# Smaller portions of top-k work beside each expert chunk (UPUMP 2.7 to 1.1) in a one-core decoder block

## The chip, the cores and the metric

The kernel runs on one core of one Trainium2 chip. A core has a matrix engine (PE; its weight loads are shown apart as PEld), three engines for elementwise work (DVE or VectorE, ACT or ScalarE, POOL or GpSimd), and a queue that only starts transfers (SP). Each engine works through its own list of instructions; semaphores tie the lists together. The metric is the time of one execution in microseconds on the device; lower is better. All compared runs use the same inputs.

## The reference

One decoder block for 512 tokens of width 1024 in float32. First come a gated MLP, a sliding window attention and a merge of the two; the change does not touch them. Then comes the PEER layer, a retrieval over 128 x 128 = 16384 experts of one neuron each, with 8 heads and 16 experts per head and token:

```python
q = (xb @ w_pq).reshape(-1, PEER_HEADS, PEER_QDIM)
q1, q2 = q[..., :PEER_HALF], q[..., PEER_HALF:]
s1 = jnp.einsum('thd,hkd->thk', q1, sub_k1)
s2 = jnp.einsum('thd,hkd->thk', q2, sub_k2)
v1, i1 = lax.top_k(s1, PEER_TOPK)
v2, i2 = lax.top_k(s2, PEER_TOPK)
cand = (v1[..., :, None] + v2[..., None, :]).reshape(-1, PEER_HEADS, PEER_TOPK * PEER_TOPK)
sc, ci = lax.top_k(cand, PEER_TOPK)
e = (take(i1, ci // PEER_TOPK) * PEER_NKEYS + take(i2, ci % PEER_TOPK))
g = jax.nn.softmax(sc, axis=-1)
act = jax.nn.gelu(jnp.einsum('thkd,td->thk', peer_u[e], xb))
return jnp.einsum('thk,thkd->td', g * act, peer_v[e])
```

A gate, a residual sum and a layer norm follow.

## The kernel before, in words

For the first 384 tokens the kernel does not gather experts. It computes the activations of all 16384 experts densely, in 128 chunks of 128 experts, and weighs them with a tensor G that is zero except at the chosen experts. A chunk has two halves. `U_chunk(i)` loads a 512 KB tile of peer_u, splits it into a high part (`hiU`, ACT, line 451) and a low part (`loU`, raw minus high), and multiplies: 24 products of 384 columns on PE, three for each of 8 slices, high by high, high by low of the tokens, and low by high (lines 63 to 65). `V_chunk(i)` loads 512 KB of peer_v, splits it in the same way (`hiV`, `loV`), forms the weighted activations `wf`, `wh`, `wl` from the activations and G, and adds 18 products of 512 columns to six accumulators (lines 776 to 780).

`load_split2` makes the low part on POOL (line 457) while `last["pool"]` is true, and on DVE (line 459) from then on. It turns false in `end_topk`, which stands in a list of background work, `bg`, behind the top-k of all heads. This list holds Python generators. `pump(us)` adds `us` to a credit and takes work from the list until the credit is used up; each step names its price in microseconds (1.02 for the best 16 of one row, for example). So the credit decides which piece of top-k is written beside which chunk in the program, and how many chunks are written before the switch.

The order of the program is: the queries and scores, with `pump(QPUMP)`; then chunks with their low parts on POOL, with `pump(UPUMP + 1.2)` each, as long as the top-k lasts, their activations sent out to DRAM (`spilled`); then 21 chunks whose activations stay in SBUF (`res`), beside which `spread()` builds G on DVE, ACT and PE (one-hot tiles `oh`, products `psg` of lines 650 and 651, `stg`) and writes it to DRAM; some more spilled chunks; then the V halves of the 21 kept chunks; then U and V of the rest, in pairs; and at the end the V halves of all spilled chunks, whose activations come back from DRAM as `ar`, four chunks at a time.

The last 128 tokens go another way, `gather()`: their experts' rows are fetched with indirect DMAs that POOL issues (`ru`, line 665, then `rv`, line 676; 128 of each), and DVE multiplies them (lines 667 and 682). These DMAs read the list of experts `idx`, which DVE writes in one instruction, line 662, at the end of top-k. The steps are handed out with `pump_gather`: GR = 1.1 for each kept chunk's V, GUV = 2.9 for each pair, and what is then left of 260, spread evenly, over the spilled chunks. A row is a 128 x 1024 float32 tile, and four are in flight.

The kernel is written through a framework that places instructions on each engine's list with an estimate of its own of when each will be ready. So a list can hold an instruction earlier than the program text has it. Of the calls that the prediction speaks of, the text has:

```python
            U_chunk(i, False)
            spilled.append(i)
            pump(UPUMP + 1.2 * bool(last.get("pool")))
```
```python
    left = 260 - n_g
            pump_gather(left / (len(spilled) - 6))
```

Of the kernel before, what the change touches and what calls it, by code (L numbers as in the profile page):

```python
# [30 lines left out]
FPOOL = {0: 2, 1: 2, 2: 0, DENSE: 0}  # L31
UPUMP = 2.7
GUV = 2.9
# [22 lines left out]
def block_kernel(ctx, tc, I, out):  # L56
# [53 lines left out]
    with ExitStack() as fr:  # L110
# [22 lines left out]

# [1 line left out]
        cs = wp.tile([P, D], F32, name="cs")  # L135
# [23 lines left out]

        # the first column blocks of the projection build up while the modulation comes in  # L160
        wf4 = Split(big(fp, "C", "w4hi"), big(fp, "D", "w4lo"))
# [15 lines left out]
        first = [I["w_k"], I["w_v"], I["w_q"][0], I["w_q"][1]]  # L177
# [21 lines left out]

# [1 line left out]
        att = ExitStack()  # L201
# [19 lines left out]

        # keys j of a block: those of the block itself where j <= q, those of the one before where j > q
        mcur = ap_.tile([P, P], F32, name="mcur")
# [66 lines left out]

# [1 line left out]
        vln = fp.tile([P, NT, D], F32, name="vln", tag="F", bufs=1)  # L292
        w = None
        for n in range(NT):
            for gh in range(4):
                attn_group(n, gh)
                u = 4 * n + gh
# [7 lines left out]
        att.close()  # L305
# [1 line left out]
        sp_ = ExitStack()  # L307
# [32 lines left out]

# [1 line left out]
        gp = fr.enter_context(tc.tile_pool(name="gp", bufs=1, reuse_waits="tile"))  # L342
        part = big(keep, "E", "part", F32)
        for j in range(NK):
# [3 lines left out]
            for i in range(16 + 4 * j, 20 + 4 * j):  # L348
# [10 lines left out]
                   gp.tile([P, NK, S], F32R, name="mTlo"))  # L359
        # rows of 1 + gt1, 1 + gt2 and h2's scale and shift: turned, then spread to all partitions by DMA  # L360
        m4 = gp.tile([P, 4, NK], F32, name="m4")
# [24 lines left out]

# [1 line left out]
        xhat = keep.tile([P, NT, D], F32, name="xhat", tag="E", bufs=1)  # L388
# [10 lines left out]
        for hh in range(2):  # L399
            for t in range(NT):  # L400
# [13 lines left out]
                for kh in range(2):  # L414
                    pt = bank("tr", 2, f"ptx{t}{kh}")
                    hf = gp.tile([P, 4, P], F32, name=f"hf{t}{kh}", tag="hf", bufs=2)
                    for k4 in range(4):
                        k = 4 * kh + k4
                        nc.tensor.transpose(pt[:, k4 * P:(k4 + 1) * P], xhat[:, t, k * P:(k + 1) * P], ident)
                    for k4 in range(4):  # L420
                        k = 4 * kh + k4
                        if k < NEV:
                            nc.scalar.activation(hf[:, k4, :], pt[:, k4 * P:(k4 + 1) * P], AF.Identity,
                                                 scale=G2c[:, k:k + 1], bias=B2c[:, k:k + 1])
# [5 lines left out]
                    nc.vector.tensor_sub(h2T.lo[dst], hf, h2T.hi[dst].bitcast(F32))  # L430
# [1 line left out]
    pw = ctx.enter_context(tc.tile_pool(name="pw", bufs=1, reuse_waits="tile"))  # L432
# [3 lines left out]
    last = {}  # L436

    def behind(ins, other):
        """keeps ins behind other in the queue of their engine"""
        tc.add_manual_dep(ins.ins, other.ins.name,  # L440
                          mybir.DependencyInfo(mybir.DependencyClass.NoSync, mybir.DependencyReason.DATA))
# [24 lines left out]

    # background work on the vector engine, given out in portions beside the dense products
    bg = []
# [10 lines left out]

# [1 line left out]
    def raw_row(nm):  # L481
# [18 lines left out]

# [1 line left out]
    tk = ExitStack()  # L502
# [34 lines left out]
    def topk(nm, n, src, dst):  # L537
        """src(half, j): the scores of lane j of n; dst(tensor): where the lanes' 16 choices go"""
        def tl(what, shape, dt):
            return tp.tile(shape, dt, name=f"{what}{nm}", tag=f"{what}_{n}", bufs=2 if n == DENSE else 1)  # L540
        v = [tl(f"v{i}", [P, n, 16], F32) for i in range(2)]
        ix = [tl(f"ix{i}", [P, n, 16], U32) for i in range(2)]
        for half in range(2):
            for j in range(n):
                top16(v[half][:, j, :], ix[half][:, j, :], src(half, j), P, f"{nm}{half}{j}")
                yield 1.02
        # candidates (a, b) in order; a pair outside the rows has 16 or more before it that are no smaller
        cand = tl("cand", [P, n, 17, 8], F32)
        nc.vector.tensor_tensor(cand[:, :, 0:2, :].rearrange("p t a b -> p t (a b)"), v[1],
                                v[0][:, :, 0:1].to_broadcast([P, n, 16]), op=ALU.add)  # L550
        nc.vector.tensor_tensor(cand[:, :, 2:17, :], v[0][:, :, 1:16].unsqueeze(3).to_broadcast([P, n, 15, 8]),
                                v[1][:, :, 0:8].unsqueeze(2).to_broadcast([P, n, 15, 8]), op=ALU.add)
        yield 0.12 + 0.14 * n
        sc = dst(scs)
        pos = tl("pos", [P, n, 16], U32)
        for j in range(n):
            top16(sc[:, j, :], pos[:, j, :], cand[:, j].rearrange("p a b -> p (a b)"), 136, f"c{nm}{j}")
            yield 1.06
        # positions to (a, b), then the keys they stand for
        r = tl("r", [P, n, 16], U32)  # L560
        ab = [tl(f"ab{i}", [P, n, 16], F16) for i in range(2)]
        nc.vector.tensor_scalar(r, pos, 3, None, op0=ALU.logical_shift_right)
        nc.vector.tensor_scalar(ab[0], r, 1, 0, op0=ALU.subtract, op1=ALU.max)
        nc.vector.scalar_tensor_tensor(ab[1], ab[0], 1.0, ab[0], op0=ALU.min, op1=ALU.add)
        nc.vector.scalar_tensor_tensor(ab[1], ab[1], -8.0, pos, op0=ALU.mult, op1=ALU.add)
        yield 0.4
        for i, to in ((0, i1s), (1, i2s)):
            ixf = tl("ixf", [P, n, 16], F16)
            nc.vector.tensor_copy(ixf, ix[i])
            oh = tl("ohl", [P, 16, n * 16], F16)  # L570
            nc.vector.tensor_tensor(oh, io16[:, :, 0:16 * n],
                                    ab[i].rearrange("p t k -> p (t k)").unsqueeze(1).to_broadcast([P, 16, 16 * n]),
                                    op=ALU.is_equal)
            o4 = oh.rearrange("p j (t k) -> p j t k", t=n)
            nc.vector.tensor_mul(o4, o4, ixf.rearrange("p t j -> p j t").unsqueeze(3).to_broadcast([P, 16, n, 16]))
            yield 0.2 + 0.42 * n
            for m in (8, 4, 2):
                nc.vector.tensor_add(oh[:, 0:m, :], oh[:, 0:m, :], oh[:, m:2 * m, :])
            nc.vector.tensor_add(dst(to), oh[:, 0, :].rearrange("p (t k) -> p t k", t=n),
                                 oh[:, 1, :].rearrange("p (t k) -> p t k", t=n))  # L580
            yield 0.2 + 0.14 * n
# [20 lines left out]

# [1 line left out]
    def spread():  # L604
# [52 lines left out]

# [1 line left out]
    wg = gat.tile([P, P], F32, name="wg")  # L659
# [83 lines left out]
    def load_G(run):  # L743
        """weights for a run of at most 8 neighbouring chunks"""
        g = vs["vp"].tile([P, SD // TG, 8, TG], F32, name=f"G{run[0]}", tag="G", bufs=2)
# [215 lines left out]
```

## Time and profile before

| what | value |
|---|---|
| time, median of 3 runs | 1770.31 us (1767.48 to 1774.57) |
| span of the profiled execution, first to last instruction | 1769.1 us |
| PE busy | 1666.7 us, 94% of the span |
| DVE, ACT, POOL busy | 1342.3, 751.4 and 450.3 us |
| moved by DMA | 413.82 MB, 234 GB/s over the span |
| granted TensorE clock, mean | 0.981 of full speed |

The profile is of one execution, and no time other than its span is given for it; the span lies 1.2 us under the median. A busy PE is not a PE at its peak, since matmuls are pipelined and overlap in the profile. An engine's idle time is shown with what ended it, and idle time of an engine that nobody waits for costs nothing.

### The profile page before, as it was taken

The page shows a single profiled execution, that of the slowest core. Times are in us where ns is not written, and L with a number is a line of the kernel's source. Part 1 is how long each engine was busy: PE and PEld are TensorE (multiplying, and loading weights), DVE is VectorE, ACT ScalarE, POOL GpSimd, SP SyncE. Part 2 cuts the span into 40 slices and gives each one's busy share as a digit, 9 for nine tenths or more (in the row PEclk, how much of TensorE's full clock was granted, in tenths as well). Part 3 has the DMA queues.
Part 4 walks back from the last instruction along what each step waited for, and adds up shares of the span by engine and source line. Part 5 has one row for each costly group of instructions (what it writes and reads, how often), then busy time and mean ns, then how long its engine had stood idle before and what let it go on. Part 6 is the DMA issues. An engine that isn't in the chain of part 4 may idle for free.

```text
span 1769.1 us, 23554 instructions
## 1 busy us (share of the span) xinstructions
PE 1666.7 (94%) x8658; PEld 1444.7 (82%) x8658; DVE 1342.3 (76%) x2483; ACT 751.4 (42%) x1171; POOL 450.3 (25%) x321
## 2 busy tenths in 40 slices
PE   5999989999999991888999999999999999999997
PEld 3866778788788991788898899999999999999886
DVE  6466786444469999787978777878878878888776
ACT  3467632233523330888843333333333333333343
POOL 2000000000133541000012444444454554554002
PEclk9999999999999995999999999999999999999999
DMA  7502267542332341656799999999989989999972
GB/s 269 189 1 72 103 217 245 190 149 83 108 104 84 131 156 35 240 211 224 257 337 334 349 319 335 349 313 343 343 305 334 356 310 347 324 322 358 296 236 76
DMA packets 164837, 413.82 MB, mean 234 GB/s; under 512 B 24849, under 2 KB 75313, under 8 KB 161394
## 3 DMA queue, kind: packets, MB, share of 16 engines
q1 hardware_dynamic: 127330, 277.79, 45.7%
q0 software_dynamic: 36960, 134.50, 21.3%
q8 instruction: 67, 1.10, 0.2%
q14 instruction: 48, 0.39, 0.1%
q10 hardware_dynamic: 432, 0.04, 0.0%
HBM read 379.04 MB, written 32.98 MB: 233 GB/s over the span
## 4 chain that ended last, share of the span: by engine, by line
PE 46%; issue 2%; DVE 1%; ACT 1%; POOL 1%; DMA 0%; DVEq 0%; POOLq 0%; ACTq 0%
PE acc L779 9%; PE acc L780 9%; PE acc L776 9%; PE psU L65 7%; PE psU L63 7%; PE psU L64 7%; ACT stg L652 1%; POOL ru L665 1%; DMA ru<-in_peer_u_dram,idx 0%; ACT oh L640 0%; DVE oh L642 0%; DVE xhat L707 0%; DVE oh L635 0%; DVE xhat L715 0%; DVE ru L667 0%
## 5 line engine op out<-in xcount | busy, mean ns | idle before, releaser
L65 PE MATMUL psU<-h2Thi,loU 128*128 128x384 f32 x1008 | 340.1, 337 | 38.0 <-DVE loU L459 38.0
L63 PE MATMUL psU<-h2Thi,hiU 128*128 128x384 f32 x1008 | 340.5, 338 | 0.0
L64 PE MATMUL psU<-h2Tlo,hiU 128*128 128x384 f32 x1008 | 339.7, 337 | 0.0
L780 PE MATMUL acc<-hiV,wl 128*128 128x512 f32 x768 | 300.3, 391 | 0.0
L779 PE MATMUL acc<-loV,wh 128*128 128x512 f32 x768 | 300.1, 391 | 0.0
L776 PE MATMUL acc<-hiV,wh 128*128 128x512 f32 x768 | 298.6, 389 | 1.2 <-ACT wh L761 1.2
L665 POOL DMA_INDIRECT ru<-in_peer_u_dram,idx x128 | 155.5, 1215 | 466.3 <-DVE ru L667 410.2
L459 DVE TENSOR_TENSOR loV<-rawV,hiV 128x1024 fp32r<-128x1024 f32 x128 | 156.6, 1224 | 117.1 <-ACT hiV L451 116.9
L451 ACT ACTIVATE hiV<-rawV 128x1024 fp32r<-128x1024 f32 x128 | 135.3, 1057 | 242.1 <-PE psU L64 224.2
L676 POOL DMA_INDIRECT rv<-in_peer_v_dram,idx x128 | 181.9, 1421 | 209.1 <-DVE facc L682 185.7
L65 PEld LDWEIGHTS psU<-h2Thi,loU 128*128 128x128 f32 x1008 | 190.5, 189 | 38.3 <-DVE loU L459 38.3
L451 ACT ACTIVATE hiU<-rawU 128x1024 fp32r<-128x1024 f32 x126 | 133.7, 1062 | 169.6 <-PE acc L780 75.2
L64 PEld LDWEIGHTS psU<-h2Tlo,hiU 128*128 128x128 f32 x1008 | 190.7, 189 | 3.0
L63 PEld LDWEIGHTS psU<-h2Thi,hiU 128*128 128x128 f32 x1008 | 190.5, 189 | 3.0
L780 PEld LDWEIGHTS acc<-hiV,wl 128*128 128x128 f32 x768 | 144.1, 188 | 30.4 <-DVE wl L762 0.3
L776 PEld LDWEIGHTS acc<-hiV,wh 128*128 128x128 f32 x768 | 144.2, 188 | 29.8 <-ACT wh L761 1.5
L779 PEld LDWEIGHTS acc<-loV,wh 128*128 128x128 f32 x768 | 144.1, 188 | 28.7 <-DVE loV L459 0.3
L682 DVE SCALAR_TENSOR_TENSOR facc<-rv,wg,facc 128x1024 f32<-128x1024 f32 x126 | 159.3, 1279 | 9.5 <-DMA rv<-in_peer_v_dram,idx 9.3
L761 ACT ACTIVATE wh<-wf 128x384 fp32r<-128x384 f32 x128 | 67.1, 526 | 216.3 <-DVE wf L757 112.8
L667 DVE SCALAR_TENSOR_TENSOR ru<-ru,h2n 128x1024 f32<-128x1024 f32 x128 | 154.3, 1221 | 5.6 <-DMA ru<-in_peer_u_dram,idx 5.6
L459 DVE TENSOR_TENSOR loU<-rawU,hiU 128x1024 fp32r<-128x1024 f32 x108 | 131.5, 1220 | 5.7 <-ACT hiU L451 5.7
L457 POOL TENSOR_TENSOR lopq<-rawpq,hipq 128x1024 fp32r<-128x1024 f32 x16 | 39.2, 2452 | 323.2 <-ACT hipq L451 323.2
(626 smaller groups left out, 2946.5 us busy)
## 6 DMA issues: line engine op xcount, KB each, us to landing
rawU<-in_uT_dram SPq DMA_DIRECT2D x128, 512.0 KB, 5.0
rawV<-in_peer_v_dram SPq DMA_DIRECT2D x128, 512.0 KB, 6.0
wa<-in_w_ada_dram SPq DMA_DIRECT2D x48, 512.0 KB, 4.3
Gd<-stg SPq DMA_DIRECT2D x24, 1024.0 KB, 3.9
G<-Gd SPq DMA_DIRECT2D x13, 1536.0 KB, 14.6
rawpq<-in_w_pq_dram SPq DMA_DIRECT2D x16, 512.0 KB, 3.7
Ad<-act SPq DMA_DIRECT2D x29, 192.0 KB, 2.8
ar<-Ad SPq DMA_DIRECT2D x7, 768.0 KB, 7.7
```

Of the source, the lines that this page charges most:

```text
L63: nc.tensor.matmul(ps, l.hi, r.hi, start=(i == 0), stop=False)
L64: nc.tensor.matmul(ps, l.hi, r.lo, start=False, stop=False)
L65: last = nc.tensor.matmul(ps, l.lo, r.hi, start=False, stop=(i == n - 1))
L451: h = nc.scalar.activation(hi, raw, AF.Copy)
L459: last["dve"] = nc.vector.tensor_sub(lo, raw, hi.bitcast(F32))
L665: nc.gpsimd.indirect_dma_start(out=rows, out_offset=None, in_=I["peer_u"], in_offset=bass.IndirectOffsetOnAxis(ap=idx[:, s:s + 1], axis=0))
L667: paced(nc.vector.scalar_tensor_tensor(rows, rows, 1.0, h2n, op0=ALU.mult, op1=ALU.mult, accum_out=wg[:, s:s + 1]))
L676: nc.gpsimd.indirect_dma_start(out=rows, out_offset=None, in_=I["peer_v"], in_offset=bass.IndirectOffsetOnAxis(ap=idx[:, s:s + 1], axis=0))
L682: paced(nc.vector.scalar_tensor_tensor(fa, rows, wg[:, s:s + 1], fa, op0=ALU.mult, op1=ALU.add))
L776: m = nc.tensor.matmul(acc, l.hi, r.hi, start=st, stop=False)
L779: nc.tensor.matmul(acc, l.hi, r.lo, start=False, stop=False)
L780: nc.tensor.matmul(acc, l.lo, r.hi, start=False, stop=sp_)
```

## The change

UPUMP, the portion of top-k work that is handed out beside each chunk of the first kind, goes from 2.7 to 1.1. With the 1.2 that is added while POOL makes the low parts, a chunk brings 2.3 of credit where it brought 3.9. So more chunks are written before `end_topk` is reached.

```diff
@@ -29,7 +29,7 @@
 NTAIL = 4
 FPOOL = {0: 2, 1: 2, 2: 0, DENSE: 0}
-UPUMP = 2.7
+UPUMP = 1.1
 GUV = 2.9
 GU = 0
 NPRE = 2
```

The other lines of the diff empty lines that held comments, and no line moves. Before, chunks 2 to 19 (18 chunks) have their low parts on POOL, 20 to 40 are kept, 50 to 127 go in pairs, and 29 are spilled. Now 2 to 31 (30 chunks) have their low parts on POOL, 32 to 52 are kept, 62 to 127 go in pairs, and 41 are spilled. Of the 256 gathered rows' steps on DVE, 8 stood behind the last U chunk, and now 43 do, beside V chunks 0 to 31, 53 and 54.

The first place is the list of POOL about the switch. Its rows before (`loU` are low parts, `ru` the first gathers; the first two rows are chunks 18 and 19):

```order
L457 TENSOR_TENSOR loU_5491<-rawU_5488,hiU_5490 128x1024
L457 TENSOR_TENSOR loU_5534<-rawU_5531,hiU_5533 128x1024
L665 DMA ru_7938<-in_peer_u_dram,idx 128x1024
L665 DMA ru_7971<-in_peer_u_dram,idx 128x1024
L665 DMA ru_8004<-in_peer_u_dram,idx 128x1024
L665 DMA ru_8037<-in_peer_u_dram,idx 128x1024
L609 IOTA ioi 128x128
```

And the same place now, where the first two rows are chunks 18 and 19 again, and the later low parts are those of chunks 20 to 23:

```order
L457 TENSOR_TENSOR loU_5375<-rawU_5372,hiU_5374 128x1024
L457 TENSOR_TENSOR loU_5421<-rawU_5418,hiU_5420 128x1024
L665 DMA ru_8346<-in_peer_u_dram,idx 128x1024
L665 DMA ru_8379<-in_peer_u_dram,idx 128x1024
L665 DMA ru_8412<-in_peer_u_dram,idx 128x1024
L457 TENSOR_TENSOR loU_5467<-rawU_5464,hiU_5466 128x1024
L665 DMA ru_8445<-in_peer_u_dram,idx 128x1024
L457 TENSOR_TENSOR loU_5513<-rawU_5510,hiU_5512 128x1024
L457 TENSOR_TENSOR loU_5562<-rawU_5559,hiU_5561 128x1024
L457 TENSOR_TENSOR loU_5609<-rawU_5606,hiU_5608 128x1024
```

The gathers have kept their place behind chunk 19, and the twelve new low parts stand behind three of them (the first) and four of them (the other eleven).

The second place is the list of DVE at the end of top-k; here are the rows before, where the `loU` are chunks 20 to 22:

```order
L579 TENSOR_TENSOR i2s<-ohll__5524 128x128
L662 SCALAR_TENSOR_TENSOR idx<-i1s,i2s 128x128
L459 TENSOR_TENSOR loU_5606<-rawU_5603,hiU_5605 128x1024
L459 TENSOR_TENSOR loU_5691<-rawU_5688,hiU_5690 128x1024
L459 TENSOR_TENSOR loU_5776<-rawU_5773,hiU_5775 128x1024
```

And now, where the `loU` are chunks 32 and 33:

```order
L579 TENSOR_TENSOR i2s<-ohll__5864 128x128
L662 SCALAR_TENSOR_TENSOR idx<-i1s,i2s 128x128
L459 TENSOR_TENSOR loU_6014<-rawU_6011,hiU_6013 128x1024
L459 TENSOR_TENSOR loU_6099<-rawU_6096,hiU_6098 128x1024
L590 TENSOR_REDUCE z<-gs 128x32
```

`idx` is the 1100th instruction of DVE in both kernels, with the same instructions ahead of it; only the chunks behind it are others.

The third place is the list of DVE in the last stage, where each row of `loV` is one spilled chunk; before:

```order
L459 TENSOR_TENSOR loV_14304<-rawV_14301,hiV_14303 128x1024
L762 TENSOR_TENSOR wl_14340<-wf_14337,wh_14339 128x384
L757 TENSOR_TENSOR wf_14402<-ar_14364,G_14234 128x384
L762 TENSOR_TENSOR wl_14375<-wf_14372,wh_14374 128x384
L757 TENSOR_TENSOR wf_14435<-ar_14364,G_14234 128x384
L459 TENSOR_TENSOR loV_14334<-rawV_14331,hiV_14333 128x1024
L682 SCALAR_TENSOR_TENSOR facc_11248<-rv_14361,wg,facc_11248 128x1024
```

And a like piece now:

```order
L459 TENSOR_TENSOR loV_14268<-rawV_14265,hiV_14267 128x1024
L682 SCALAR_TENSOR_TENSOR facc_11656<-rv_14295,wg,facc_11656 128x1024
L682 SCALAR_TENSOR_TENSOR facc_11655<-rv_14298,wg,facc_11655 128x1024
L762 TENSOR_TENSOR wl_14347<-wf_14344,wh_14346 128x384
L459 TENSOR_TENSOR loV_14304<-rawV_14301,hiV_14303 128x1024
L682 SCALAR_TENSOR_TENSOR facc_11656<-rv_14331,wg,facc_11656 128x1024
```

Each chunk of the last stage has one or two gathered rows beside it now, where about one chunk in three had one.

## Rows read from the trace of the kernel before

**Rows 1.** The page: busy tenths of PE in 40 equal slices of the span.
```profile
PE   5999989999999991888999999999999999999997
```
**Rows 2.** Waits of PE: us in total, times, longest, the two largest.
```profile
PE psU L65 <- DVE loU L459: 38.0, 1, 38.0
PE psg L650 <- DVE oh L642: 23.0, 17, 2.6
```
**Rows 3.** Waits of POOL, the one that idx ended.
```profile
POOL ru L665 <- DVE idx L662: 46.7, 1, 46.7
```
**Rows 4.** Two stretches of the stall: busy PE, PEld, DVE, ACT, POOL; clock.
```profile
660.00:680.00 20.00, 3.86 (x23) 3.51 (x22) 19.97 (x131) 3.20 (x5) 0.00 (x0) 0.66 0.00 0
680.00:700.00 20.00, 0.00 (x0) 0.00 (x0) 19.58 (x69) 0.63 (x1) 0.00 (x0) 0.50 0.00 0
```
**Rows 5.** Timeline of PE at both ends of the stall: start, duration, instruction.
```profile
663.52 0.33 PE L64 MATMUL psU<-h2Tlo,hiU 128*128 128x384 f32 x1
701.83 0.69 PE L65 MATMUL psU<-h2Thi,loU 128*128 128x384 f32 x1 [37.98 <-DVE loU L459]
```
**Rows 6.** Timeline of DVE where top-k ends.
```profile
700.35 0.29 DVE L662 SCALAR_TENSOR_TENSOR idx<-i1s,i2s 128x128 int32<-128x128 f32 x1
700.56 3.49 DVE L459 TENSOR_TENSOR loU<-rawU,hiU 128x1024 fp32r<-128x1024 f32 x3
```
**Rows 7.** Timeline of POOL about the stall.
```profile
647.70 2.41 POOL L457 TENSOR_TENSOR loU<-rawU,hiU 128x1024 fp32r<-128x1024 f32 x1 [1.75 <-ACT hiU L451]
651.86 2.40 POOL L457 TENSOR_TENSOR loU<-rawU,hiU 128x1024 fp32r<-128x1024 f32 x1 [1.75 <-ACT hiU L451]
...
700.92 1.76 POOL L665 DMA_INDIRECT ru<-in_peer_u_dram,idx  x1 [46.66 <-DVE idx L662]
702.99 1.89 POOL L665 DMA_INDIRECT ru<-in_peer_u_dram,idx  x1 [0.30 <-issue]
705.19 1.38 POOL L665 DMA_INDIRECT ru<-in_peer_u_dram,idx  x1 [0.31 <-issue]
```
**Rows 8.** Busy time while G is built: PE, PEld, DVE, ACT, POOL.
```profile
711.00:877.00 166.00, 142.63 (x1294) 136.24 (x1293) 135.73 (x129) 144.89 (x242) 0.00 (x0) 0.98 0.61 227
```
**Rows 9.** DMA issues: count, KB each, median us to landing.
```profile
rawV<-in_peer_v_dram SPq DMA_DIRECT2D x128, 512.0 KB, 6.0
...
G<-Gd SPq DMA_DIRECT2D x13, 1536.0 KB, 14.6
...
ar<-Ad SPq DMA_DIRECT2D x7, 768.0 KB, 7.7
```
**Rows 10.** Stretches with much DMA; the last three are clock, DMA share, GB/s.
```profile
900.00:940.00 40.00, 40.00 (x185) 34.03 (x185) 32.21 (x47) 14.93 (x20) 10.41 (x10) 1.00 1.01 349
...
1620.00:1640.00 20.00, 20.00 (x101) 17.93 (x100) 17.10 (x21) 8.42 (x12) 8.45 (x6) 1.00 0.98 370
```
**Rows 11.** Groups of DVE, 1690 to 1735 us: busy us, mean ns.
```profile
L459 DVE TENSOR_TENSOR loV<-rawV,hiV 128x1024 fp32r<-128x1024 f32 x12 | 14.6, 1219 | 0.6 <-ACT hiV L451 0.6
L762 DVE TENSOR_TENSOR wl<-wf,wh 128x384 fp32r<-128x384 f32 x12 | 6.7, 556 | 10.2 <-ACT wh L761 10.2
L757 DVE TENSOR_TENSOR wf<-ar,G 128x384 f32<-128x384 f32 x11 | 6.1, 555 | 0.5 <-DMA ar<-Ad 0.3
L682 DVE SCALAR_TENSOR_TENSOR facc<-rv,wg,facc 128x1024 f32<-128x1024 f32 x2 | 2.6, 1279 | 0.0
```
**Rows 12.** Timeline of DVE: low parts of two V chunks in a row.
```profile
1695.20 1.22 DVE L459 TENSOR_TENSOR loV<-rawV,hiV 128x1024 fp32r<-128x1024 f32 x1
...
1699.28 1.22 DVE L459 TENSOR_TENSOR loV<-rawV,hiV 128x1024 fp32r<-128x1024 f32 x1
```
**Rows 13.** Timelines, the last V tile: its load on SP, its low part on DVE.
```profile
1729.09 0.33 SPq L448 DMA_DIRECT2D rawV<-in_peer_v_dram  x1
...
1744.05 1.23 DVE L459 TENSOR_TENSOR loV<-rawV,hiV 128x1024 fp32r<-128x1024 f32 x1 [0.39 <-ACT hiV L451]
```

## The prediction

> **What bounds the kernel now.** I read the page's 40 slices first: PE is busy nine tenths or more nearly everywhere, with one hole at the 16th slice [rows 1]. So the kernel is bound by PE, and a change is worth what it adds to or takes from PE's waits, since the number of products stays (9022 rows in PE's list in both kernels). The waits of PE, read second, show two that matter here: one single wait of 38.0 us for a low part made by DVE, and 17 waits of together 23.0 us for one-hot tiles while G is built [rows 2]. The hole is the first of them. The stretches show it: from 660 to 700 us DVE is busy throughout and PE hardly at all, and the granted clock falls from full to 0.50, the lower of its two levels (1.2 GHz) [rows 4]. PE stops at 663.52 after the high products of chunk 20 and goes on at 701.83 [rows 5]. The timeline of DVE says why: the low part of chunk 20 is the first that DVE makes, and DVE's list has all of top-k ahead of it, whose last instruction is `idx` at 700.35 [rows 6]. POOL, which had made a low part every 4.16 us until then, stood idle meanwhile: its next instruction was the first gather, which waited 46.7 us for the same `idx` [rows 3, 7].
>
> **What the change aims at, and what stands in its way.** Twelve more chunks with their low parts on POOL are 12 x 4.16 = 49.9 us of PE work [rows 7], more than the 38.0 us hole. If POOL could make them while DVE ends top-k, the hole would close. But the order of POOL's list shows three gathers ahead of chunk 20's low part, and the gathers wait for `idx`. The wait of 46.66 us in front of the first gather [rows 7] is just the proof that such a wait holds POOL's list. DVE's list up to `idx` is the same 1100 instructions, and up to 654 us nothing on POOL, PE or ACT differs, so `idx` again ends at 700.35 + 0.29 = 700.64. So I expect the hole to stay, with another name: PE waits for POOL's `loU`, and POOL waits for DVE's `idx`.
>
> **The switch, counted out.** After `idx` come the three gathers, 700.92 to 705.19 + 1.38 = 706.57, then a gap of 0.3 as between them, then chunk 20's low part on POOL, 2.40 us [rows 7]: ready at 709.3. Before, DVE had it ready at 700.56 + 1.22 = 701.78 (one low part lasts 1.22 us), and PE started at 701.83 [rows 5, 6, 11]. So PE goes on 7.5 us later. After that POOL needs 2.4 us for each chunk (and one more gather, under 2 us) against PE's 4.16, so the other eleven cost nothing; if POOL were to fall behind, each would cost its excess over 4.16. DVE stands still meanwhile, since its next instruction, chunk 32's low part, waits for a high part whose buffer (three in turn) PE frees only some chunks earlier; behind it are the softmax and the building of G, and PE has 12 chunks to do before it needs those. What is late next is the building of G, by about the same time as PE.
>
> Part of the 7.5 us may come back there. In that stage ACT is busy 144.89 of 166 us [rows 8] and PE waits 23.0 us for what DVE and ACT make [rows 2], so PE isn't what paces it. In the list of PE 21 chunks now stand between the first and the last product of G, where 20 stood: one more chunk of 4.16 us lies beside a stage that others pace. If all of it hides in PE's waits, 7.5 - 4.2 = 3.3 us are left; if none, 7.5. I take 5, about the middle.
>
> The spilled chunks are 12 more: 12 more stores and loads of activations of 192 KB. The stores fall into a stretch in which the DMA share is low (0.00 in the hole [rows 4]) and cost nothing. The chunk pairs lose 12, and with them 12 x 2.9 = 35 gathered rows, which move to the last stage; the pairs that stay are the same.
>
> **The last stage, counted out.** It has 34 chunks beside which 43 rows are gathered. Per chunk that is 512 KB of V, 1536 / 8 = 192 KB of G, 768 / 4 = 192 KB of activations [rows 9], and 43 / 34 x 512 = 648 KB of rows: 1544 KB, or 1.58 MB. PE takes 4.08 us for a V chunk (distance of two low parts [rows 12]). So it asks for 387 GB/s, over 34 x 4.08 = 138.7 us. The trace shows 370 GB/s in 20 us at the entry to this stage, and 349 over 40 us in which the DMA share reached 1.01, both with PE fully busy [rows 10]. For 53.7 MB these rates give 145.2 and 154.0 us: 6.5 or 15.3 us more than PE. Against it stands a lead: the last V tile's load is issued 15.0 us before its low part starts, and lands in 6.0 [rows 9, 13], so some 9 us of lateness can be eaten up before PE feels it. DVE needs 1.22 + 0.56 + 0.56 + 43 / 34 x 1.28 = 3.95 us of the 4.08 per chunk [rows 11], so it just fits and can make up nothing. Bounds: 0 (6.5 under 9) and 15.3 (the lower rate, no lead). I take 2, near the lower one, since the rate of 370 was reached just at the entry to this stage.
>
> The Trainium skill has a rule on this ("DMA: Bandwidth & Descriptors", section "Where 436 GB/s comes from"): for transfers between HBM and SBUF the HBM side binds at about 358 GB/s per core. The 370 of this trace is already above it, over 20 us. By the rule the last stage would be DMA bound, an estimate of 150 us, 11.4 more than PE's; less the lead that is 2.4, and the sum would barely move.
>
> **Sum.** The profiled span of 1769.1 us is 1.2 under the median of 1770.31, and I carry the difference along: 1770.3 + 5 + 2 = 1777.3 us, 0.4% more. What can be told from no change here is about 0.5%, or 8.9 us.
>
> **Rivals.**
> *The hole closes (faster).* If POOL gets to chunk 20's low part before 664 us, because the gathers don't hold it, PE runs on with 49.9 us of work against 38.0 us of hole. Then 38.0 us go, and 2 come at the end: 1734 us. For it speaks that POOL is idle and 49.9 is more than 38.0; against it, the row in which a gather held POOL for 46.66 us. It decides if `idx` is ready before about 654 us, and nothing in the change makes it so. Chance 0.08.
> *The last stage is bound by DMA (slower by more).* At 349 GB/s and with no lead left, because the pairs ahead of it already run DMA near its limit: 1770.3 + 7.5 + 15.3 = 1793 us. For it: the demand of 387 is above every stretch of the trace. Against: the lead. It decides where the rate stays under 53.7 MB / (138.7 + 9) = 364 GB/s. Chance 0.15.
> *All of it is hidden.* The building of G takes up what it can and the last stage costs nothing: 1770.3 + 0 to 3.3, some 1772 us. For it: 23.0 us of PE's waits there are three times what is to be hidden. Against: this stage is only one chunk longer. Chance 0.20.
>
> **How the numbers follow.** The forecast has 0.57; its own range goes from 3.3 + 0 to 7.5 + 6.5 us above before, 1773.6 to 1784.3. Slower by over 0.5% means above 1779.2: four tenths of the forecast's 0.57, and the DMA rival, 0.38. Faster by over 0.5%: the closed hole, and 0.02 for a luckier interleaving while G is built, 0.10. The rest, 0.52, is no change. The range of 8 in 10 reaches from 1765 (the hidden case, less 5 us for the spread of the runs of before, 1767.48 to 1774.57) to 1793 (the DMA rival); it leaves out the closed hole and half of what lies at the ends.
>
> **What would show it.** The first row of PE's waits should read about 45.5 us, once, with POOL's `loU` (line 457) as the releaser instead of DVE's; POOL should wait about 47 us for `idx` in front of the first gather, with 18 chunks' low parts ahead of it and 12 behind. The one-hot waits should be under 23.0 us. In the last stage the rate should be 360 to 390 GB/s and PE's waits for low parts or `wl` a few microseconds. The prediction is wrong if the 38 us are gone, or if PE waits over 9 us in the last stage.

## The result, and the profile after

The changed kernel takes 1795.61 us (median of 4 runs, 1792.75 to 1802.82), the kernel before 1770.55 us on the same chip (1767.48 to 1774.57). The ratio is 1.0154, 95% interval [1.0137, 1.0171]: 1.5% slower. 1777.3 was forecast, and the range ended at 1793. The profiled execution, the fastest of the four, took 1792.75 us with a span of 1789.9 us, 20.8 us more than the span before; the medians differ by 25.1 us.

The page's slices of PE differ in a few digits, and two places matter: the hole at the 16th slice is still there, and the 38th slice, a nine before [rows 1], is an eight.

```profile
PE   6999999999999982988899999999999999999897
```

PE's waits (total us, times, longest) answer to [rows 2]:

```profile
PE psU L65 <- POOL loU L457: 43.2, 1, 43.2
PE psg L650 <- DVE oh L642: 21.5, 18, 2.3
PE acc L779 <- DVE loV L459: 13.1, 6, 5.6
...
PE acc L776 <- ACT wh L761: 4.0, 1, 4.0
```

The hole is 5.2 us longer and has the other name, the waits for one-hot tiles are 1.5 us shorter, and two rows have come up: 17.1 us for low parts and `wh` of V chunks, where 1.2 us stood. They carry most of the loss.

**The switch.** POOL's timeline answers to [rows 7], and PE's row to [rows 5]:

```profile
699.65 1.03 POOL L665 DMA_INDIRECT ru<-in_peer_u_dram,idx  x1 [46.62 <-DVE idx L662]
700.99 0.96 POOL L665 DMA_INDIRECT ru<-in_peer_u_dram,idx  x1 [0.30 <-issue]
702.25 0.94 POOL L665 DMA_INDIRECT ru<-in_peer_u_dram,idx  x1 [0.31 <-issue]
703.21 2.35 POOL L457 TENSOR_TENSOR loU<-rawU,hiU 128x1024 fp32r<-128x1024 f32 x1
```
```profile
705.61 0.69 PE L65 MATMUL psU<-h2Thi,loU 128*128 128x384 f32 x1 [43.21 <-POOL loU L457]
```

The steps are those forecast: POOL held 46.62 us by the first gather, three gathers, then chunk 20's low part, then PE. Only the gathers took 2.9 us together where they took 5.0 before.

**Where the 20.8 us are.** The views of the lines 65 and 780 end with the start of the first and of the last product; here first those of the kernel before, from 1450 us on and of the whole span:

```profile
L65 PE MATMUL psU<-h2Thi,loU x176: 334/334/343, 1454.1 to 1632.2; 128*128 128x384 f32 x176
L780 PE MATMUL acc<-hiV,wl x768: 388/389/498, 905.8 to 1758.8; 128*128 128x512 f32 x192
```

And those of the changed kernel:

```profile
L65 PE MATMUL psU<-h2Thi,loU x128: 334/334/343, 1453.3 to 1581.5; 128*128 128x384 f32 x128
L780 PE MATMUL acc<-hiV,wl x768: 387/389/628, 956.3 to 1779.5; 128*128 128x512 f32 x192
```

After its last U product each kernel has only V chunks left, six products of line 780 each: 258 / 6 = 43 now, 186 / 6 = 31 before. Twelve V chunks are 12 x 4.08 = 49.0 us of PE [rows 12]. So up to the last U product the changed kernel is 50.7 - 49.0 = 1.7 us *ahead* (its execution was 1.4 us ahead when PE stopped, at 662.40), and from there on it loses 198.0 - 126.6 - 49.0 = 22.4 us. The whole loss is in the last stage.

**The last stage.** Here is what DVE waits for in front of `wf` (total us, times, longest), and the time from issue to landing of the activations `ar`, in the kernel before (the 7.7 of [rows 9] leaves out the one short load):

```profile
DVE wf L757 <- DMA ar<-Ad: 6.0, 3, 3.7
```
```profile
DMA to landing us min/median/max: 4.4/7.0/9.6
```

And now, from 1560 us on:

```profile
DVE wf L757 <- DMA ar<-Ad: 26.8, 6, 7.6
```
```profile
DMA to landing us min/median/max: 3.4/9.3/13.5
```

And here one such wait, followed through the timelines of SP, DVE and PE:

```profile
1652.81 7.71 SPq L448 DMA_DIRECT2D rawV<-in_peer_v_dram  x3
1660.58 0.43 SPq L888 DMA_DIRECT2D ar<-Ad  x1
...
1665.14 0.55 DVE L762 TENSOR_TENSOR wl<-wf,wh 128x384 fp32r<-128x384 f32 x1
1673.29 0.56 DVE L757 TENSOR_TENSOR wf<-ar,G 128x384 f32<-128x384 f32 x1 [7.60 <-DMA ar<-Ad]
1673.77 1.22 DVE L459 TENSOR_TENSOR loV<-rawV,hiV 128x1024 fp32r<-128x1024 f32 x1
...
1675.04 0.80 PE L779 MATMUL acc<-loV,wh 128*128 128x512 f32 x1 [5.59 <-DVE loV L459]
```

The request for `ar` leaves SP only when the rawV ahead of it has got its buffer. By the chain of work it takes 12.6 us to land, but DVE has reached the `wf` that needs it after 5.1 us and stands there. Behind `wf` on DVE's list is a low part that PE waits for, and behind that the low parts that free buffers for more rawV. All six waits are of this kind: in their groups DVE stood at the first `wf` 4.7 to 8.2 us after the request had left SP, and `ar` landed 8.2 to 13.5 us after it. PE waited 12.6 us for low parts behind five of them; the sixth of its waits, 0.5 us, stands by itself.

The 4.0 us for `wh` are of another kind. They stand at the entry to the stage, and the chain of work leads from them back to a V tile (start, duration, piece):

```profile
1568.45 18.06 DMA rawV<-in_peer_v_dram
1586.62 1.06 ACT hiV L451
1587.70 0.44 DVE loV L459
...
1590.01 0.80 PE acc L776
```

This tile was asked for 0.5 us after a load of G, 1536 KB, and landed after 18.1 us, where the median of a V tile had been 6.0 [rows 9].

The stretches show what follows: the rate stays below the 387 GB/s that were asked for, and PE's clock falls with its stall (columns as in [rows 10]). From 1660 us on the DMA share falls with it, as SP sends three requests for rawV over 14.7 us; from 1640 us on it does not (1.01), though 317 GB/s were moved.

```profile
1600.00:1620.00 20.00, 20.00 (x90) 16.54 (x89) 17.81 (x25) 8.05 (x11) 8.48 (x6) 1.00 1.05 391
1620.00:1640.00 20.00, 17.87 (x79) 14.52 (x78) 13.48 (x16) 7.38 (x10) 4.99 (x4) 1.00 0.94 331
1640.00:1660.00 20.00, 18.75 (x84) 15.16 (x83) 17.36 (x21) 5.90 (x8) 8.11 (x7) 1.00 1.01 317
1660.00:1680.00 20.00, 14.41 (x57) 11.47 (x56) 12.33 (x16) 4.65 (x6) 4.63 (x5) 0.83 0.83 312
```

Of the 22.4 us, 17.1 are PE's waits. Most of the rest are slower products behind them, where the clock has fallen: the products of V chunks last 394 to 397 ns in the mean here, and 389 or 390 before, which makes 4.6 us over 258 products on each of three lines.

### The profile page after: what moved, and what is told of

Read it like the earlier page. It is cut to its first block, busy times and chain, and to the rows that moved or that the text cites. A ratio compares the mean times of both kernels' runs of the same rounds, so it can differ in the third digit from the quotient of the medians.

```text
span 1789.9 us, 23603 instructions
## 1 busy us (share of the span) xinstructions
PE 1669.7 (93%) x8658; PEld 1443.7 (81%) x8658; DVE 1324.9 (74%) x2471; ACT 750.7 (42%) x1171; POOL 478.8 (27%) x333
## 4 chain that ended last, share of the span: by engine, by line
PE 41%; DMA 4%; DVE 3%; ACT 1%; issue 1%; SPq 0%; DVEq 0%; ACTq 0%
PE acc L779 8%; PE acc L780 8%; PE acc L776 8%; PE psU L65 6%; PE psU L63 6%; PE psU L64 6%; DMA ar<-Ad 2%; DMA rawV<-in_peer_v_dram 1%; DVE loV L459 1%; DVE facc L682 1%; ACT stg L652 0%; DVE wl L762 0%; DVE oh L642 0%; DMA rawU<-in_uT_dram 0%; DVE xhat L707 0%
## 5 line engine op out<-in xcount | busy, mean ns | idle before, releaser
L65 PE MATMUL psU<-h2Thi,loU 128*128 128x384 f32 x1008 | 339.2, 337 | 43.2 <-POOL loU L457 43.2
L779 PE MATMUL acc<-loV,wh 128*128 128x512 f32 x768 | 302.0, 393 | 13.1 <-DVE loV L459 13.1
L459 DVE TENSOR_TENSOR loU<-rawU,hiU 128x1024 fp32r<-128x1024 f32 x96 | 117.1, 1220 | 61.3 <-ACT hiU L451 61.2
## 6 DMA issues: line engine op xcount, KB each, us to landing
G<-Gd SPq DMA_DIRECT2D x14, 1536.0 KB, 14.7
```

The lines of the kernel that those rows point to most:

```text
L65: last = nc.tensor.matmul(ps, l.lo, r.hi, start=False, stop=(i == n - 1))
L459: last["dve"] = nc.vector.tensor_sub(lo, raw, hi.bitcast(F32))
L779: nc.tensor.matmul(acc, l.hi, r.lo, start=False, stop=False)
```

## The experiments

Two theories of the last stage stood against each other at first: *rate* (the transfers bring too little) and *DVE* (DVE has 3.95 of 4.08 us to do per chunk and can make nothing up). A third came up on the way: *lead* (`ar` is asked for too late, whatever DVE and the rate are). The theory of the hole was the gathers' place on POOL. Each run's own kernel before is the base of its ratio. A difference in us to the changed kernel compares medians from different chips, on which the kernel before took 1768.89 to 1771.53 us, so it can be off by some 2 us.

### The switch

**e1_hold**: the first four gathers stand behind the last low part that POOL makes.

```diff
-            nc.gpsimd.tensor_sub(lo, raw, hi.bitcast(F32))
+            last["plo"] = nc.gpsimd.tensor_sub(lo, raw, hi.bitcast(F32))
...
-            nc.gpsimd.indirect_dma_start(out=rows, ...
+            d = nc.gpsimd.indirect_dma_start(out=rows, ...
+            if s < 4:
+                behind(d, last["plo"])
```

> The changed kernel, with one edit: the first four gathers are kept behind the last low part in POOL's list. Theory A (the hole of 43.2 us at the switch is kept open by the gathers that hold POOL's list): the hole goes, since POOL then has 49.9 us of chunks for PE; the time falls by 40 to 46 us against the changed kernel, to about 1752 us, with the waits of the last stage (17 us) left as they are. Rival (the hole is DVE's top-k itself, or POOL and DVE hinder each other so that chunks on POOL come late): the time falls by under 15 us, and PE waits for POOL's low parts several times.

Measured: 1753.60 us, ratio 0.9907 [0.9882, 0.9932]; 42.0 us under the changed kernel. The row of the hole is gone from PE's waits. POOL's timeline:

```profile
693.60 2.41 POOL L457 TENSOR_TENSOR loU<-rawU,hiU 128x1024 fp32r<-128x1024 f32 x1 [1.75 <-ACT hiU L451]
...
701.91 3.37 POOL L457 TENSOR_TENSOR loU<-rawU,hiU 128x1024 fp32r<-128x1024 f32 x1 [1.24 <-ACT hiU L451]
712.99 1.76 POOL L665 DMA_INDIRECT ru<-in_peer_u_dram,idx  x1 [7.70 <-DVE idx L662]
```

So the twelve low parts cover the end of top-k once nothing stands ahead of them. The last stage's waits stayed (DVE 31.4 us on `ar`).

### The last stage

**e3_early**: `ar` of the next group is asked for behind the first chunk of the running group; the buffers are the same two.

```diff
             if (j - run[0]) % 4 == 0:
-                ar = ...; d = nc.sync.dma_start(ar[:, 0:n, :], ...); behind(d, last["dma"])
+                ar = arq.pop(0)
             V_chunk(j, ar[:, (j - run[0]) % 4, :], n_v)
+            if (j - run[0]) % 4 == 0 and groups:
+                load_ar()
```

> The changed kernel; in the last stage the next four chunks' activations are asked for behind the first chunk of a group instead of behind its last. The same bytes move. Theory C (lead): DVE's 26.8 us of waits for these activations go, and with them most of PE's 17 us; about 1780 us. Theory B (rate): the lateness moves to V tiles or gathered rows; the time falls by under 5 us.

Measured: 1782.49 us, ratio 1.0075 [1.0052, 1.0099]; 13.1 us under the changed kernel. DVE waits for `ar` no more, and PE's waits in the last stage are 7.6 us: 3.1 for `wh` at the entry, 3.5 for one high part at 1668 us, 1.0 for others. ACT, which makes the high parts, waits 38.5 us for V tiles from 1560 us on, where it waited 18.4 in the changed kernel and 0.9 before. So part of the lateness did move to the V tiles, as *rate* has it, while the larger part of the waits is gone. From 1600 to 1660 us PE is busy throughout, at 373 GB/s:

```profile
1600.00:1660.00 60.00, 60.00 (x266) 49.70 (x265) 55.06 (x67) 21.55 (x30) 27.93 (x20) 1.00 1.04 373
```

**e8_nomul** and **e9_nofetch** part DVE's share from the transfers' share. In e8 the last 43 rows are fetched, but only 16 of their 1024 columns are multiplied; in e9 they are not fetched, and the multiplications read an older row.

```diff
+                c = slice(0, 16 if s >= P - 43 else D)
-                paced(nc.vector.scalar_tensor_tensor(fa, rows, ...
+                paced(nc.vector.scalar_tensor_tensor(fa[:, c], rows[:, c], ...
```
```diff
+            if s < P - 43:
                 rows = gat.tile([P, D], F32, name=f"rv{s}", tag="rows", bufs=4)
                 nc.gpsimd.indirect_dma_start(out=rows, ...
```

> The changed kernel, in which the last 43 rows of peer_v are fetched as before but only 16 of their 1024 columns are multiplied and added (the other columns of these rows are left out of the sum). Transfers stay, and DVE's need per chunk of the last stage falls from 3.95 to 2.3 + 0.1 = 2.4 us of 4.08. If DVE without spare time is what makes the loads late (the raw buffers come free with DVE's low parts, and ar is issued behind them), the DVE waits on ar fall from 26.8 to under 8 us and PE's waits in the last stage from 17.1 to under 5: 1776 to 1781 us. If the transfers' rate is what makes them late, the waits stay above 12 us and the time within 1790 to 1797.

> The changed kernel, in which the last 43 rows of peer_v are not fetched, and the multiplications that stand for them read the last row that was fetched (so the sum has wrong rows in it). DVE's work stays at 3.95 of 4.08 us per chunk; the demand on transfers falls from 387 to 225 GB/s. If the transfers' rate is the cause, all of the last stage's waits go: 1776 to 1779 us. If DVE without spare time is the cause, the loads are still issued as late, but land in about 6 to 7 us where they took 9.3: DVE's waits on ar fall by a third to a half, PE keeps 6 to 12 us of waits, 1783 to 1790 us.

Measured: e8 1796.40 us, ratio 1.0135 [1.0104, 1.0165], as slow as the changed kernel; e9 1778.82 us, ratio 1.0037 [1.0020, 1.0053], 16.8 us under it. The waits of e8 on DVE from 1580 us on, and on PE:

```profile
DVE wf L759 <- DMA ar<-Ad: 52.6, 7, 8.3
```
```profile
PE acc L781 <- DVE loV L459: 13.7, 7, 3.5
PE acc L778 <- ACT wh L763: 5.1, 1, 5.1
```

From 1580 to 1740 us DVE was busy 123.7 us in the changed kernel (the third of the busy times) and 82.7 us in e8 (its eight stretches added up):

```profile
1580.00:1740.00 160.00, 143.39 (x615) 116.69 (x614) 123.69 (x148) 52.37 (x71) 54.06 (x41) 0.97 0.98 339
```
```profile
sum 160.00, PE 141.19 PEld 113.76 DVE 82.67 ACT 50.52 POOL 42.79; mean PE 17.65 PEld 14.22 DVE 10.33 ACT 6.32 POOL 5.35
```

So *DVE* falls: with a third less to do it only reaches the same `wf` sooner (4.0 to 6.0 us after the request, in its seven waits) and waits twice as long. In e9 DVE has no wait for `ar`, though four groups have no more than 5.9 to 6.1 us between request and `wf`, and PE waits 0.9 us in the last stage, the entry among it. So the transfers of the rows are needed for the loss. Both results are what was expected for *rate*: they part it from *DVE*, but not from *lead*, which neither of these two expectations names. But e3 had shown that about half of the loss can go with all rows fetched. For the waits on `ar` that leaves *lead*. The list of DVE in the changed kernel says how long it is (wf, loV and wl with their chunk's number):

```
L459 TENSOR_TENSOR loV15_14304<-rawV15_14301,hiV15_14303 128x1024
L682 SCALAR_TENSOR_TENSOR facc1_11656<-rv105_14331,wg_3455,facc1_11656 128x1024
L757 TENSOR_TENSOR wf18_14410<-ar16_14336,G16_14334 128x384
L762 TENSOR_TENSOR wl17_14380<-wf17_14377,wh17_14379 128x384
L757 TENSOR_TENSOR wf19_14446<-ar16_14336,G16_14334 128x384
L459 TENSOR_TENSOR loV16_14341<-rawV16_14338,hiV16_14340 128x1024
L682 SCALAR_TENSOR_TENSOR facc0_11655<-rv106_14368,wg_3455,facc0_11655 128x1024
L762 TENSOR_TENSOR wl18_14413<-wf18_14410,wh18_14412 128x384
L757 TENSOR_TENSOR wf20_14481<-ar20_14473,G16_14334 128x384
```

On SP `ar20` stands behind rawV19, whose buffer loV15 frees. On DVE wf20 stands seven instructions behind loV15: 2 x 1.28 + 1.22 + 4 x 0.56 = 6.0 us [rows 11], against a landing of 9.3. Without the two facc (e8) the lead is 3.5 us. The framework has put wf20 ahead of loV17, while the low part of its own chunk is loV20.

**e12_late_wf** tests that alone: the requests stay, and `wf` of a spilled chunk is kept behind the low part of the chunk ahead.

```diff
+        prev = last["dve"]
...
-        nc.vector.tensor_mul(wf..., a..., g)
+        m = nc.vector.tensor_mul(wf..., a..., g)
+        if "ar" in vs:
+            behind(m, prev)
```

> The changed kernel, in which DVE's multiplication wf of a spilled chunk is kept behind the low part loV of the chunk ahead of it in DVE's list. The requests on SP stay as and where they were. In the changed kernel wf of a new group of four stands 7 instructions, 6.0 us of DVE's work, behind the low part that lets SP ask for its ar (landing 9.3 us in the median); now it stands 19 instructions and about 15 us behind it. If the place of wf in DVE's list is what makes the lead too short, the DVE waits on ar fall from 26.8 to under 5 us and PE's waits in the last stage from 17.1 to under 8: 1779 to 1785 us, as with the earlier request. If the transfers simply bring too little in the last stage, the waits move to rawV and rows, and the time stays at 1790 to 1797. A third way: wf so late leaves ACT's wh and DVE's wl no time, and PE waits for these: over 1797.

Measured: 1779.55 us, ratio 1.0057 [1.0039, 1.0076]; 16.1 us under the changed kernel, with all rows fetched and multiplied. DVE waits for `ar` no more, since every group now has 11.8 us or more from the request to its first `wf`; PE waits 5.5 us for V chunks, 3.1 of them at the entry. And the rate that *rate* had denied is there for 120 us:

```profile
1600.00:1720.00 120.00, 120.00 (x530) 99.15 (x529) 104.35 (x123) 43.91 (x57) 53.77 (x35) 1.00 1.04 378
```

How much of the 22.4 us each run leaves can be counted as above, from the last U product to the last V product less 126.6 and 49.0 us: 27.4 in e8, 13.0 in e3, 8.9 in e12 and 1.5 in e9. So the place of `ar`'s request or use is worth 9 to 14 of the 22.4 us. What is left in e3 and e12 is gone in e9, without the rows' transfers, and in both ACT waits longer for V tiles than in the changed kernel (38.5 and 28.9 us, in e9 5.0).

**e5_before_rows** (the kernel before with GUV 2.65: 30 rows behind DVE's last `loU`, where by this count 11 stood before and 46 in the changed kernel; the switch untouched) and **e6_before_early** (the kernel before with e3's edit) ask from the other side.

> The kernel before with GUV 2.65 where it was 2.9: 30 rows stand behind the last U chunk, beside 23 V chunks, where 8 stood; the switch to VectorE stays where it was (38.0 us hole). If rows in the last stage alone make its waits, DVE waits 15 to 25 us for ar and PE 5 to 15 us there, with the hole and the one-hot waits as before: 1776 to 1787 us. If the waits of the last stage need the later switch (more chunks spilled), PE stays without waits there and the time within 0.3% of before.

> The kernel before with the edit on the activations alone: those of the next four chunks asked for behind the first chunk of the running four. There DVE waits 6.0 us for ar in the last stage, and PE only 1.2 us for what follows from it. If the late request costs only where rows are gathered beside the V chunks, nothing is to be had: 1768 to 1772 us. Rival (the late request is a fault of the program in any case, and the half clock behind a wait adds to it): 1762 to 1767 us.

Measured: e5 1779.26 us, ratio 1.0038 [1.0021, 1.0055], with 6.7 us of PE's waits for low parts in the last stage, where none stood, and the hole at 38.0 us; e6 1770.19 us, ratio 1.0004 [0.9987, 1.0021]. So rows moved into the last stage cost time with no change at the switch, and the early request is worth nothing where few rows stand there. The profile of e5 is of its slowest execution, 1785.85 us. DVE waited there 4.9 us for `ar` by name, and 8.3 us more in front of the first `wf` of two other groups, where the trace names no releaser: 13.2 us in all, short of the 15 to 25 expected. Its waits for high parts are 13.5 us, and were 10.3 before.

### How many rows go where

**e2_rows**: the changed kernel with GUV 3.42, so that 12 rows stand behind DVE's last `loU`, where 46 stood (the 43 leave out three beside the V of the last pairs), and the rest beside the pairs. **e4_all**: this with e1's and e3's edits.

```diff
-GUV = 2.9
+GUV = 3.42
```

> The changed kernel with GUV = 3.42 instead of 2.9: 12 gathered rows stand behind the last U chunk, where 46 stood, and the chunk pairs carry 34 more. Theory B (the last stage lacks DMA rate: 387 GB/s asked for): the pairs then ask for about 369 GB/s, near the same limit, so the waits move to the pairs in good part; the time falls by under 8 us. Theory C (the last stage lacks lead: its activations are asked for too late, and DVE, busy with gathered rows, has no slack to wait for them): the 17 us of waits in the last stage go and none come in the pairs; about 1778 us.

> The three edits together (gathers held behind the low parts, GUV = 3.42, activations asked for earlier). Theories A and C: hole and last-stage waits both gone, 1795.6 - 43 - 2 - 17 = about 1733 us, faster than the kernel before by about 2%. With A and B: about 1745 us.

Measured: e2 1811.59 us, ratio 1.0239 [1.0216, 1.0262]; e4 1768.95 us, 0.9992 [0.9966, 1.0019], its runs from 1758.05 to 1776.26, far over what was expected. Waits of PE for low parts have come up in the pairs, and the wait at the entry to the last stage, at 1626 us in e2, has grown to 9.2 us in both; in e2:

```profile
PE psU L65 <- DVE loU L459: 21.0, 15, 3.4
PE acc L776 <- ACT wh L761: 9.8, 2, 9.2
```
```profile
1100.00:1200.00 100.00, 97.53 (x489) 87.65 (x488) 82.61 (x124) 34.19 (x46) 52.57 (x40) 1.00 0.99 362
...
1400.00:1500.00 100.00, 93.52 (x456) 84.72 (x455) 81.52 (x82) 32.42 (x44) 55.89 (x38) 0.97 0.94 339
```

A pair with 3.42 rows asks for 512 + 512 + 192 + 3.42 x 512 = 2967 KB in 4.16 + 4.08 us, 369 GB/s. Less than that was moved, while e12 moved 378 with a demand of 387. Whether a rate or another late request holds the pairs was not tried.

### The best version

**e7_hold_early** is e1's and e3's edits on the changed kernel, **e10_hold_early_rows** this with GUV 3.1, and **e11_hold_early_u15** with UPUMP 1.5.

> Both single edits on the changed kernel at once: the first four gathers kept behind the last low part on POOL, and the activations of the next four chunks asked for behind the first chunk of the running four; GUV stays at 2.9. The two cures lie 900 us apart, so if each takes away a wait of its own they add: 1753.6 - (1795.6 - 1782.5) = 1740.5 us, 0.983 of before, with no wait of PE on a low part at the switch and no DVE wait on ar over 2 us in all. Rival (the transfers are short of bandwidth in the last stage, and an earlier ar only moves the wait to the V tiles): PE's waits in the last stage stay at 15 us or more under other names, and the time stays at 1748 to 1754.

> Both single edits on the changed kernel, with GUV 3.1 where it was 2.9: 30 rows stand behind the last U chunk, where 43 did. A pair then asks for 216 KB of rows more in ten, 348 GB/s where it was 335, over 66 pairs that moved 331 to 344 GB/s with PE never waiting; with GUV 3.42 (369 GB/s) PE waited 21 us there. If the limit lies between 350 and 369, PE's waits in the last stage fall from 8.9 to under 4 us and the time to 1736 to 1740 us. If it lies under 348, PE waits for low parts in the pairs: 1743 to 1752 us.

> Both single edits on the changed kernel, with UPUMP 1.5 where it was 1.1: 26 chunks (2 to 27) have their low parts on POOL, 37 are spilled, and 31 rows stand behind the last U chunk. POOL then has 8 chunks, 33 us, for the end of top-k, which lasts 37 us from the same place and longer where POOL works beside it (the last low part of 30 was done at 701.9 and idx came at 712.7). So PE should wait about 12 to 20 us for VectorE's first low part; the last stage gives back 4 to 6 us: 1748 to 1760 us. Rival (12 chunks were more than was needed, and three low parts in the buffers cover the rest): no wait at the switch, 1736 to 1740 us.

Measured: e7 1742.54 us, ratio 0.9822 [0.9793, 0.9850]; e10 1745.71, 0.9880 [0.9850, 0.9910], its runs from 1738.09 to 1751.74; e11 1743.44, 0.9860 [0.9844, 0.9877]. The two cures add (42.0 + 13.1 = 55.1 expected, 53.1 found), and the kernel is 1.8% faster than before. The other two settings are no faster; whether they are a few tenths of a per cent slower the runs leave open, as the three intervals overlap or touch. That leaves e10's question open too, since its median lies in the range of one of its theories and its fastest run in that of the other. In e11 PE waits 11.8 us at the switch for DVE's first low part, and not at all in the last stage: what four chunks fewer on POOL cost there, the last stage gave back, the wait at its entry included.

## Why the prediction was wrong

**The hole: right.** It stayed, 43.2 us for 45.5 forecast, with POOL's `loU` as the releaser, POOL waiting 46.6 us for `idx`. e1 shows the cause: with the gathers moved behind the low parts, 42.0 us went. The rival "the hole closes" named the right condition, and the change didn't meet it.

**What the hole costs: the mechanism right, the size too high.** The forecast's term was 5 us, bounds 3.3 and 7.5. PE waited 5.2 us longer, as the gathers took 2.1 us less than in [rows 7]. The last product of G starts at 926.5 us where it started at 876.1 (the last start in each row, first that of before):

```profile
L651 PE MATMUL psg<-oh,oh x384: 217/218/308, 717.4 to 876.1; 128*128 128x128 f16 x192
```
```profile
L651 PE MATMUL psg<-oh,oh x384: 217/218/308, 766.4 to 926.5; 128*128 128x128 f16 x192
```

With 12 x 4.16 = 49.9 us of chunks more ahead of it, that is 0.5 us later, or 2 if the 1.4 us are counted by which this execution was ahead. The rest of the 5.2 us hid in the building of G, as argued there, and by the last U product nothing of it was left.

**The last stage: the step that failed.** It is the term of 2 us, and the lead that it rests on: "Against it stands a lead [...] some 9 us of lateness can be eaten up before PE feels it" and "I take 2". The trace has 22.4 us, and PE's waits there are 17.1, past the 9 that the prediction itself named as the sign of being wrong. The lead was read off one V tile [rows 13], and the activations, whose landing of 7.7 us stood in [rows 9], were counted as bytes only. They have a lead of their own, 6.0 us of DVE's list in the group shown and 4.7 to 8.2 us in the six that waited, and it is shorter than their landing. In the kernel before PE lost nothing by it, and e6 shows that nothing was to be had: DVE had time to spare there, standing 10.2 us for ACT's `wh` from 1690 to 1735 [rows 11]. With one or two rows beside each chunk the landing went from 7.0 to 9.3 us, DVE met the wait in six groups, and each wait held the low parts behind it: 12.6 of the 17.1 us. Another 4.0 are the V tile at the entry, for which the 9 us to spare were not enough: it took 18.1 us to land in place of 6.0.

Two runs take away the waits on `ar` with all transfers and all of DVE's work in place (e3 asks earlier, e12 uses later: 13 and 16 us of the time), and the run with less work on DVE (e8) takes away none. That DVE's work "just fits and can make up nothing" was therefore not what cost the time. e9, without the rows' transfers, takes away 17 us, the entry's wait among them.

**The rate: wrong as a bound.** The rival of 1793 us was nearest in time, and its number for the decision (under 364 GB/s) was met: 55.60 MB from 1580 to 1745 us are 337 GB/s. But this rate was no limit, since e12 moved 378 GB/s over 120 us with PE fully busy, above every stretch on which the forecast rested [rows 10]. The DMA share doesn't show a limit either: over 1580 to 1740 us it was 0.98 in the changed kernel, at 339 GB/s, and 1.04 in e12's stretch. The rival was right in one thing, that V tiles too come late with the rows beside them. The Trainium skill has the HBM side bind at about 358 GB/s per core for transfers between HBM and SBUF ("DMA: Bandwidth & Descriptors", section "Where 436 GB/s comes from"), a figure that it gets by dividing a stack's 716 GB/s by two cores. The 378 of e12 are above it, so it was no bound for this kernel on one core; the measurement decides.

**What stays open.** e9 and e12 end at 1778.8 and 1779.6 us, 7 and 9 us over their kernels before. In e12 8.9 us of the last stage's loss are left, with 5.5 us of waits, the most of them at the entry (3.1 us for one `wh`). In e9's profile 1.9 us are lost up to the last U product, 1.5 in the last stage, and 4.9 behind the last product (15.2 us where 10.3 follow before), all of them behind the request for the last store. Why the V tile at the entry took 18.1 us, and how much of it the load of G ahead of it has to do with, no run took apart.

## What to carry to other kernels

For each load count the lead as well as the bytes: find on the queue what the request waits for, find on the consumer's list how much work lies between that release and the first use, and set this against the landing time under the *new* load. Look for it above all where a load serves several steps at once, since the framework may have put its first use far ahead of the work that it belongs to. And when more work is to flow past a switch, look at what already stands on that engine's list ahead of it; one instruction that waits takes the whole gain.

## What the runs showed that was not expected

While POOL makes low parts, single instructions of DVE can become as long as one of POOL's. In e1_hold:

```profile
698.33 2.49 DVE L565 SCALAR_TENSOR_TENSOR ab1l__5780<-ab1l__5780,posl__5593 128x128 f16<-128x128 f16 x1
```

The same instruction took 0.28 us in the kernel before, where POOL stood idle at that time. Seven instructions between 656 and 706 us last 0.6 to 2.2 us longer than in the kernel before, 11.9 us together, and `idx` came at 712.42 us in place of 700.35. Each of the seven ran beside a low part on POOL; six have two tensor inputs, one (line 563) has one. For the six this agrees with the Trainium skill ("SBUF — State Buffer", section "🔬 SBUF: two separate sides"): DVE with two SBUF inputs and a GpSimd operation that reads SBUF exclude each other for a whole instruction. So the end of top-k comes later as POOL has more to do, and twelve more chunks were not too many for a hole of 38.0 us: with eight, in e11, `idx` came at 705.39 and PE waited 11.8 us.
